# Moving SBUF tiles so that streamed weights start 64 bytes (mod 256) past the moving operand, in a two-layer hybrid decoder trunk

## The chip, the cores and the metric

The kernel runs on one core of one Trainium2 chip. The metric is device time in microseconds (us), the median of several executions. A profile of one further execution stands beside it.

## The reference

Two layers act on a sequence of 256 tokens of width 1024, in float32. Each layer is a half-step SwiGLU feed-forward, three parallel token mixers (differential attention, RWKV-7, HGRN2), and a second half-step SwiGLU, each on a normalized and modulated input:

```
for l in range(DEPTH):                                   # 2 layers
    mod = (silu(c) @ mod_w[l] + mod_b[l]).reshape(9, D)
    u = rms_norm(h, norm_w[l, 0]) * (1 + m[1]) + m[0]
    h = h + 0.5 * m[2] * (silu(u @ w_gate) * (u @ w_up)) @ w_down     # 1024 -> 2816 -> 1024
    u = rms_norm(h, norm_w[l, 1]) * (1 + m[4]) + m[3]
    p = u @ w_in[l]                                                    # 1024 -> 8480
    y = g_a * attention(p) @ w_out_a + g_b * rwkv7(p) @ w_out_b + g_c * hgrn2(p) @ w_out_c
    h = h + m[5] * (y @ w_out[l])
    u = rms_norm(h, norm_w[l, 2]) * (1 + m[7]) + m[6]
    h = h + 0.5 * m[8] * (second SwiGLU of u)
```

## The kernel before

Activations lie transposed, 128 features on the partitions and the 256 tokens along the row, so a matrix product is a chain of TensorE matmuls with a 128x128 block of weights as the stationary operand and a 128x256 block of activations as the moving operand. For precision each weight and each activation is split into a high and a low part (`split`, L364 to L366), and three of the four products are summed: helper `mm3` (L356 to L362) issues, for eight blocks k, high weights times high activations, high weights times low activations, and low weights times high activations, 24 matmuls in one accumulation. Nearly every matmul is followed by one with another block of weights, so a weight load (PEld in the profile) stands between any two; the load for the next matmul runs while the present one streams its moving operand.

Weights are never reused: `load` (L1323) brings 512 KB by the SP queue into one of four buffers `raw`, ScalarE makes `wh` (L365), VectorE makes `wl` (L366), three buffers each. The items are worked off in one fixed list: per layer the feed-forward (22 gate and 22 up blocks, then 8 down blocks in three pieces), the mixer's projections in the order of a string, its output projections and `w_out`, then the second feed-forward. Mixer work of other kinds is interleaved by a budget per item.

The moving operands of `mm3`, by their names in the profile:

- `zh`, `zl`: the activations before their normalization is known, 258 columns wide (two columns carry the shift), eight blocks in one tile, so a block starts 1,032 bytes after the one before. They serve the first items of each feed-forward and of each mixer.
- `uh`, `ul`: the normalized input, 256 columns (1,024 bytes) a tile, 3,072 of these passes' matmuls in the four feed-forwards and 1,920 in the two mixers.
- `hh`, `hl`: the hidden activations of a feed-forward, 528 matmuls in each.
- `oa`, `ob`, `oc`, then `yh`, `yl`: outputs of the three mixers and their gated sum; 192 matmuls each for the three, 384 for the sum.

In five projections (L945 to L947, `tm_proj`) the roles are exchanged: the activations are stationary and 512 columns of weights move.

SBUF tiles come from pools, stacked in the order in which they are opened: constants, residual and `zh`/`zl`, `stream` (`raw`, `wh`, `wl`), `tmp` (pool `tp`), and above it either pool `ff` of a feed-forward or pool `mx` of a mixer. In a pool, tiles lie in the order of their first use, each rounded up to 32 bytes. What a tile's address is mod 256 therefore follows from all that was placed ahead of it. In the built program every block of `wh` and `wl` starts at 224 mod 256.

Of the kernel before, what the change touches and what calls it, by code (L numbers as in the profile page):

```python
# [10 lines left out]
F32 = mybir.dt.float32  # L11
# [11 lines left out]
S = 256  # L23
KT = D // 128
# [6 lines left out]
NC = S // C  # L31
# [32 lines left out]
def trunk(ctx: ExitStack, tc: tile.TileContext, A, out):  # L64
# [6 lines left out]
    tp = ctx.enter_context(tc.tile_pool(name="tmp", bufs=2))  # L71
# [4 lines left out]
    def psd(w=S):  # L76
        return pd.tile([128, w], F32, name="psd", tag="psd")
# [27 lines left out]
    cos = cp.tile([128, 2, 32], F32, name="cos")  # L105
    sin = cp.tile([128, 2, 32], F32, name="sin")
    lam_init = [0.8 - 0.6 * math.exp(-0.3 * l) for l in range(L)]

    def col(l, n, i=0, w=1):
        o, _ = COLS[n]  # L110
        return cols[:, l, o + i:o + i + w]
# [138 lines left out]
    NOW = {}  # L250
# [92 lines left out]
    def mods_due(r, t=None):  # L343
        if t and mod_todo.index(t) < mod_pos[0]:
            return
        NOW["mods"] = NOW.get("mods", 0.0) + r
        while NOW["mods"] >= 1:
            NOW["mods"] -= 1
            mod_step()
# [65 lines left out]
    def z_close():  # L415
        with ahead(PRIO["z"]):
            z_sums()
# [14 lines left out]
    def z_rstd():  # L432
        pr = psm([128, S])
        PE.matmul(pr, ones, NOW["dg"].rearrange("p b t -> p (b t)"), start=True, stop=True)
        SC.copy(rstd, pr)
# [7 lines left out]
    def ffn_open():  # L443
        es = NOW["es"] = ExitStack()
        fp = NOW["ff"] = es.enter_context(tc.tile_pool(name="ff", bufs=1))
        cbc = NOW["cbc"] = fp.tile([128, D], F32, name="cbc")
        load_c(cbc)
# [15 lines left out]
    def ffn(l, i, nxt, per):  # L463
        s = 2 * i
        hid = [None] * FT
        pp = {}
        def gate_up(f, j, wh, wl):
            if f == 0 and j == 0 and (l or i):
                ffn_open()
            fp = NOW["ff"]  # L470
            if f >= (MODF if l + i else MODF0):
                mods_due(per[0])
            nz = NZ0 if l + i == 0 else NZ
            zt = f < nz
            if f == 0 and j == 0:
                NOW["z"] = [(NOW["zh"][:, k], NOW["zl"][:, k]) for k in range(KT)]
            n = 2 * f + j
            if n == 0:
                NOW["u"] = []
            if wh is None:  # L480
                p = NOW["pre"][n]
            else:
                p = psd(S + 2 if zt else S)
                mm3(p, wh, wl, NOW["z"] if zt else NOW["u"], late=n == 0)
                if n == 0:
                    z_close()
                elif n == 1:
                    z_rstd()
            if zt:
                make_u(l, s, fp, [k for k in range(KT) if (k * (2 * nz - 1)) // KT + 1 == n])  # L490
            pp[j] = p
            if j == 0:
                return
            pg, pu = pp[0], pp[1]
            t1 = fp.tile([128, S], F32, name="t1", tag="t1", bufs=2)
            t2 = fp.tile([128, S], F32, name="t2", tag="t2", bufs=2)
            if zt:
                bt = fp.tile([128, 1], F32, name="bt", tag="bt", bufs=2)
                V.tensor_copy(bt, pg[:, S:S + 1])
                V.tensor_mul(t1, pg[:, 0:S], rstd)  # L500
                SC.activation(t1, t1, AF.Silu, bias=bt)
                V.tensor_mul(t2, pu[:, 0:S], rstd)
                V.scalar_tensor_tensor(t2, t2, pu[:, S:S + 1], t1, ALU.add, ALU.mult)
            else:
                SC.activation(t1, pg, AF.Silu)
                V.tensor_mul(t2, t1, pu)  # L506
            a1 = fp.tile([128, S], F32R, name=f"hh{f}")
            a2 = fp.tile([128, S], F32R, name=f"hl{f}")
            split(a1, a2, t2)
            hid[f] = (a1, a2)  # L510

        def down(f, k0, kn, wh, wl):
            if f == 0 and k0 == 0:
                mod_until(l, 3 * s + 2)
                if nxt:
                    z_open(*nxt)
            if f < MODD:
                mods_due(per[1])
            if k0 == 0:
                pp[0] = psd()  # L520
            p = pp[0]
            mm3(p, wh, wl, hid[k0:k0 + kn], first=k0 == 0, last=k0 == 16)
            if k0 == 16:
                V.scalar_tensor_tensor(h[f], p, modd[:, l, 3 * s + 2, f:f + 1], h[f], ALU.mult, ALU.add)
                if nxt:
                    z_tile(*nxt, f)
                else:
                    nc.sync.dma_start(out[f], h[f])
                if f == KT - 1:
                    if i == 0:  # L530
                        mod_until(l, MODM[l])
                        NOW["ff"] = NOW["cbc"] = None
                    NOW["es"].close()

        for f in range(FT):
            for j in range(2):
                add(A["gu"][l, i, f, j], D, partial(gate_up, f, j))
        for f in range(KT):
            for k0, kn in ((0, 8), (8, 8), (16, 6)):
                add(A["dn"][l, i, f][:, k0 * 128:(k0 + kn) * 128], kn * 128, partial(down, f, k0, kn))  # L540
# [7 lines left out]
    def mixer(l):  # L548
        M = {}

        def tile_(shape, name, tag=None, dt=F32, bufs=None):
            kw = {} if bufs is None else {"bufs": bufs}
            return M["mx"].tile(shape, dt, name=name, tag=tag or name, **kw)


        def r_open():
            es = M["es"] = ExitStack()
            M["mx"] = es.enter_context(tc.tile_pool(name="mx", bufs=1))
            M["lw2"] = tile_([128, 512], "lw2", "Xa")
            GP.dma_start(M["lw2"], A["wa2"][l])  # L560
            GP.dma_start(rows, A["rows"][:, l * NROW:(l + 1) * NROW].to_broadcast([128, NROW]))
            M["u"] = None
            for n, t in (("rr", "r"), ("kk", "k"), ("aa", "a")):
                M[n] = tile_([128, 4, S], n, t)
            M["vv"] = tile_([128, 4, C + S], "vv", "v")
            M["Za"] = tile_([128, 2, NC, 2, 128], "Za")
            M["Zb"] = tile_([128, 2, NC, 2, 128], "Zb")
            M["H"] = tile_([128, 4, NC, 128], "H")
            M["EC"] = tile_([128, 4, NC], "EC")


        def shift_out(o, p, mi, b=None):
            ts = tile_([128, S + 1], "ts", bufs=2)
            if b is None:
                GP.memset(ts[:, 0:1], 0.0)
                SC.activation(ts[:, 1:S + 1], p, AF.Copy, scale=col(l, "mu", mi))
            else:
                SC.mul(ts[:, 0:1], b, omu[:, l, mi:mi + 1])
                SC.activation(ts[:, 1:S + 1], p, AF.Identity, scale=col(l, "mu", mi), bias=b)
            V.scalar_tensor_tensor(o, p, omu[:, l, mi:mi + 1], ts[:, 0:S], ALU.mult, ALU.add)  # L580
            return ts
# [6 lines left out]
        def proj(evac, wh, wl):  # L588
            n = M.setdefault("n", 0)
            M["n"] += 1  # L590
            zt = n < NZM
            if n == 0:
                r_open()
                drain("C")
                M["z"] = [(NOW["zh"][:, k], NOW["zl"][:, k]) for k in range(KT)]
                NOW["u"] = M["u"] = []
                M["wait"] = []
            mix_mods()
            p = psd(S + 2 if zt else S)
            mm3(p, wh, wl, M["z"] if zt else M["u"], late=n == 0)  # L600
            if n == 0:
                z_close()
            elif n == 1:
                z_rstd()
            if zt:
                make_u(l, 1, M["mx"], [k for k in range(KT) if (k * (NZM - 1)) // KT + 1 == n])
            M["wait"].append((evac, p))
            while n and M["wait"]:
                f, p = M["wait"].pop(0)
                bt = None  # L610
                if zt:
                    bt = tile_([128, 1], "bt", bufs=2)
                    SC.copy(bt, p[:, S:S + 1])
                    pn = tp.tile([128, S], F32, name="pn", tag="sq")
                    V.tensor_mul(pn, p[:, 0:S], rstd)
                    p = pn
                f(p, bt)
# [722 lines left out]
    z_open(0, 0)  # L1340
    step("C")
    pre = NOW["pre"] = [psd(S + 2) if i < 4 else psm([128, S + 2]) for i in range(NI)]
    zf = NOW["ff"].tile([128, KT, S + 2], F32, name="zf")
    zh, zl = NOW["zh"], NOW["zl"]
    raws = []
    for t in range(KT):
# [108 lines left out]
```

## Time and profile before

| | us |
|---|---|
| median of 3 timed executions | 1498.49 (1496.09 to 1505.21) |
| profiled execution, whole | 1506.07 |
| its span, first to last instruction | 1504.4 |
| TensorE matmul busy in it | 1449.7 (96%) |
| TensorE weight load busy | 1379.7 (92%) |
| VectorE busy | 1202.0 (80%) |
| ScalarE busy | 800.7 (53%) |
| GpSimd busy | 140.8 (9%) |

Busy time on PE is the union of modelled durations, and a matmul's modelled duration reaches over the start of the next. The time from one matmul's start to the next (its pace, below) is what a stream of matmuls costs; it comes from the length of a stretch in which PE is never idle, divided by the matmuls that start in it. A count in a stretch includes about two that began earlier and reach into it.

### The profile page before, as it was taken

How to read it: one execution, taken by the hardware profiler on the slowest of the kernel's cores; microseconds unless marked ns; L12 is line 12 of the kernel's file. 1: busy time of each engine (PE TensorE's matmuls, PEld its weight loads, DVE VectorE, ACT ScalarE, POOL GpSimd, SP SyncE). 2: the span in 40 equal slices, each digit the busy share in tenths (PEclk: the TensorE clock that was granted, in tenths of full speed). 3: DMA queues.
4: the chain of work that ended last, by engine and by line, in shares of the span. 5: the costliest groups of instructions: out<-in, count | busy, mean ns of one | idle time of the engine just before them, and what ended most of it. 6: DMA issues, size and time to landing. Idle time of an engine off the chain costs nothing. (4 is left out here: it accounts for less than half of the span.)

```text
span 1504.4 us, 30080 instructions
## 1 busy us (share of the span) xinstructions
PE 1449.7 (96%) x11848; PEld 1379.7 (92%) x11848; DVE 1202.0 (80%) x2228; ACT 800.7 (53%) x1367; POOL 140.8 (9%) x230
## 2 busy tenths in 40 slices
PE   4999999998999999999999999999979999999998
PEld 2999999997878999999999999999867789999998
DVE  5998988869779998888888888787778788886543
ACT  3564447863355656444455444688423664564432
POOL 6000010021300020000100000001222001100000
PEclk9999999999999999999999999999978999999999
DMA  9789975453326667899878997544541235665563
GB/s 329 260 271 344 319 272 176 129 173 118 116 84 197 204 205 269 287 308 308 260 267 297 327 329 256 186 141 141 164 144 46 85 127 181 200 210 184 181 189 118
DMA packets 90208, 315.92 MB, mean 210 GB/s; under 512 B 10577, under 2 KB 13009, under 8 KB 90066
## 3 DMA queue, kind: packets, MB, share of 16 engines
q1 hardware_dynamic: 86690, 308.32, 61.7%
q0 software_dynamic: 1600, 4.20, 1.1%
q8 instruction: 93, 1.52, 0.4%
q10 hardware_dynamic: 1776, 1.48, 0.3%
q14 instruction: 49, 0.40, 0.1%
HBM read 311.86 MB, written 2.10 MB: 209 GB/s over the span
## 5 line engine op out<-in xcount | busy, mean ns | idle before, releaser
L365 ACT CAST wh<-raw 128x1024 fp32r<-128x1024 f32 (+1 forms) x440 | 454.8, 1034 | 457.4 <-PE psd L362 258.0
L366 DVE TENSOR_TENSOR wl<-raw,wh 128x1024 fp32r<-128x1024 f32 (+1 forms) x440 | 533.7, 1214 | 124.8 <-ACT wh L365 119.4
L362 PE MATMUL psd<-uh,wl 128*128 128x256 f32 x1664 | 236.7, 284 | 16.6 <-DVE wl L366 16.6
L362 PE MATMUL psd<-uh,wh 128*128 128x256 f32 x1664 | 239.8, 285 | 0.0
L362 PE MATMUL psd<-ul,wh 128*128 128x256 f32 x1664 | 236.3, 284 | 0.0
L362 PEld LDWEIGHTS psd<-uh,wl 128*128 128x128 f32 x1664 | 215.0, 190 | 18.2 <-DVE wl L366 17.2
L362 PEld LDWEIGHTS psd<-uh,wh 128*128 128x128 f32 x1664 | 215.1, 189 | 4.3 <-issue 2.0
L362 PEld LDWEIGHTS psd<-ul,wh 128*128 128x128 f32 x1664 | 214.9, 190 | 0.5 <-issue 0.3
L314 DVE SCALAR_TENSOR_TENSOR mw<-mw,cbc 128x1024 f32<-128x1024 f32 x134 | 167.7, 1254 | 0.0
L362 PE MATMUL psd<-hl,wh 128*128 128x256 f32 x704 | 100.3, 282 | 0.0
L362 PE MATMUL psd<-hh,wl 128*128 128x256 f32 x704 | 100.0, 282 | 0.0
L362 PE MATMUL psd<-hh,wh 128*128 128x256 f32 x704 | 99.8, 282 | 0.0
L362 PEld LDWEIGHTS psd<-hl,wh 128*128 128x128 f32 x704 | 91.1, 188 | 0.0
L362 PEld LDWEIGHTS psd<-hh,wh 128*128 128x128 f32 x704 | 90.9, 188 | 0.0
L362 PEld LDWEIGHTS psd<-hh,wl 128*128 128x128 f32 x704 | 90.9, 188 | 0.0
L412 POOL TENSOR_TENSOR acc<-acc,sq 128x256 f32<-128x256 f32 x36 | 30.1, 835 | 605.3 <-ACT sq L410 605.0
L362 PE MATMUL psd<-zh,wh 128*128 128x258 f32 x448 | 66.0, 289 | 0.0
L946 PE MATMUL psd<-wl,uh 128*128 128x512 f32 x160 | 65.3, 408 | 0.6 <-DVE wl L366 0.6
L362 PE MATMUL psd<-zh,wl 128*128 128x258 f32 x448 | 64.9, 283 | 0.0
L506 DVE TENSOR_TENSOR t<-t,psd 128x256 f32<-128x256 f32 x64 | 26.9, 421 | 47.4 <-PE psd L362 46.5
L945 PE MATMUL psd<-wh,uh 128*128 128x512 f32 x160 | 64.7, 405 | 0.0
L947 PE MATMUL psd<-wh,ul 128*128 128x512 f32 x160 | 64.7, 404 | 0.0
(427 smaller groups left out, 2107.2 us busy)
## 6 DMA issues: line engine op xcount, KB each, us to landing
raw<-in_gu SPq DMA_DIRECT2D x176, 512.0 KB, 4.5
mw<-in_modw SPq DMA_DIRECT2D x134, 512.0 KB, 5.3
raw<-in_wfm SPq DMA_DIRECT2D x94, 512.0 KB, 3.6
raw<-in_dn SPq DMA_DIRECT2D x64, 512.0 KB, 4.7
raw<-in_wtm SPq DMA_DIRECT2D x40, 512.0 KB, 4.0
raw<-in_dn SPq DMA_DIRECT2D x32, 384.0 KB, 3.8
raw<-in_wo SPq DMA_DIRECT2D x24, 512.0 KB, 3.8
raw<-in_wout SPq DMA_DIRECT2D x16, 512.0 KB, 3.5
```

Of the source, the lines that this page charges most:

```text
L314: ins = V.scalar_tensor_tensor(w, w, 1.0, NOW["cbc"], ALU.mult, ALU.mult, accum_out=modd[:, l, j, f:f + 1])
L362: PE.matmul(p, w[:, sl[k]], xs[k][x], start=first and i == 0, stop=last and i == 3 * n - 1)
L365: SC.copy(dst_h, src)
L366: V.tensor_sub(dst_l, src, dst_h.bitcast(F32))
L412: GP.tensor_add(NOW["acc"], NOW["acc"], sq)
L506: V.tensor_mul(t2, t1, pu)
L945: PE.matmul(ps[b], u[k][0][:, ts_], w1, start=k == 0, stop=False)
L946: PE.matmul(ps[b], u[k][0][:, ts_], w2, start=False, stop=False)
L947: PE.matmul(ps[b], u[k][1][:, ts_], w1, start=False, stop=k == KT - 1)
```

## The change

The instructions and their order on every engine are the same before and after, row by row; only addresses change, and with them a few dependences that hang on what lay at an address earlier: the wait for a handful of long finished GpSimd-queue DMAs moves from the copy of `bt` to the neighbouring instruction on VectorE (twice) and from that copy to an activation on ScalarE (once).

Five edits shift tiles. An unused tile of 224 bytes, `gap`, opens pool `tmp`, so that everything behind it moves up by 224. The tiles `bt`, `ts` and `EC`, whose sizes are no multiples of 256 bytes, go from `ff` and `mx` into `tmp`. The tile `zf`, 8,256 bytes, is allocated with 8,448 bytes (33 times 256). And the name `PX` gets its 8,192 bytes when `mx` is opened instead of later.

```diff
+    tp.tile([128, 56], F32, name="gap", bufs=1)
...
-                bt = fp.tile([128, 1], F32, name="bt", tag="bt", bufs=2)
+                bt = tp.tile([128, 1], F32, name="bt", tag="bt")
...
-            M["EC"] = tile_([128, 4, NC], "EC")
+            M["EC"] = tp.tile([128, 4, NC], F32, name="EC", tag="EC", bufs=1)
+            tile_([128, 2, 4, S], "PX")
...
         def shift_out(o, p, mi, b=None):
-            ts = tile_([128, S + 1], "ts", bufs=2)
+            ts = tp.tile([128, S + 1], F32, name="ts", tag="ts")
...
-                    bt = tile_([128, 1], "bt", bufs=2)
+                    bt = tp.tile([128, 1], F32, name="bt", tag="bt")
...
-    zf = NOW["ff"].tile([128, KT, S + 2], F32, name="zf")
+    zf = NOW["ff"].tile([128, 33 * 64], F32, name="zf")[:, 0:KT * (S + 2)].rearrange("p (k s) -> p k s", k=KT)
```

The following table is counted from the addresses in the two built programs. For two consecutive matmuls of `mm3` it takes the distance, mod 256 bytes, from the moving block of the first to the weight block of the second, which is loaded while the first runs.

| moving operand | matmuls | distance before | distance after |
|---|---|---|---|
| `uh`, `ul` in the first feed-forward | 624 | 96 (seven blocks of eight), 160 (one) | 64 |
| `hh`, `hl` in the first feed-forward | 528 | 96 | 64 |
| `uh`, `ul` in the other three | 2,448 | 160 (seven blocks of eight), 224 (one) | 64 |
| `hh`, `hl` in the other three | 1,584 | 160 | 64 |
| `uh`, `ul` in the mixers | 1,920 | 32 (six of eight), 160 (two) | 64 |
| `yh`, `yl` | 384 | 32 (six of eight), 160 (two) | 64 |
| `ob` | 192 | 32 | 64 |
| `oc` | 192 | 64 | 64 |
| `oa` | 192 | 224 | 64 |
| `zh`, `zl` | 1,344 | 8 to 128 in steps of 8 | the same |
| weights, 512 wide (`tm_proj`) | 480 | 96 or 224 | 192 |

## The prediction

> **What bounds the kernel now.** The page comes first: which engine is busy, and whether at full clock.
>
> ```profile
> span 1504.4 us, 30080 instructions
> PE 1449.7 (96%) x11848; PEld 1379.7 (92%) x11848; DVE 1202.0 (80%) x2228; ACT 800.7 (53%) x1367; POOL 140.8 (9%) x230
> PE   4999999998999999999999999999979999999998
> DVE  5998988869779998888888888787778788886543
> PEclk9999999999999999999999999999978999999999
> DMA  9789975453326667899878997544541235665563
> ```
>
> PE is full in nearly every slice, at full clock except around slice 31. So the pace of its matmuls sets the time, and a change of addresses can act only there, as no instruction is added, removed or moved. The next view is the busy time in stretches with one kind of moving operand each: `zh` of the first feed-forward, its `uh`, its `hh`, then `uh` and `hh` of the second, `uh` of the third, `uh` and `hh` of the last, one `zh` stretch more.
>
> ```profile
> core 0: us, PE busy (x), PEclk, DMA share, GB/s
> 60.00:80.00 20.00, 20.00 (x169) 1.00 0.90 325
> 88.10:161.60 73.50, 73.50 (x625) 1.00 0.91 319
> 161.90:218.40 56.50, 56.50 (x478) 1.00 0.89 306
> 603.00:700.00 97.00, 97.00 (x814) 1.00 0.90 304
> 700.50:757.50 57.00, 57.00 (x478) 1.00 0.81 264
> 795.30:892.50 97.20, 97.20 (x816) 1.00 0.92 323
> 1339.50:1436.80 97.30, 97.30 (x817) 1.00 0.58 183
> 1437.00:1500.00 63.00, 63.00 (x527) 1.00 0.54 159
> ...
> 776.00:794.00 18.00, 18.00 (x151) 1.00 0.87 302
> ```
>
> PE never idles in any of them. Two of each count began earlier and are taken off; the length by the rest is the pace: 118.0 ns and 118.7 ns in the first feed-forward (`uh`, `hh`), 119.5, 119.7, 119.4, 119.4 and 120.0 in the later ones, 119.8 and 120.8 for `zh`. All are the same instruction at the same clock; what differs is where the operands lie, and the DMA share doesn't go with it (0.92 and 0.58 give the same 119.4). The same shape in the mixer's output projections stands in time order:
>
> ```profile
> 523.12 0.64 PE L362 MATMUL psd<-oc,wh 128*128 128x256 f32 x4
> ...
> 534.43 0.63 PE L362 MATMUL psd<-oa,wh 128*128 128x256 f32 x4
> ...
> 545.63 0.63 PE L362 MATMUL psd<-yh,wh 128*128 128x256 f32 x4
> ```
>
> From the first `oc` to the first `oa` are 11.31 us, from there to the first `yh` 11.20 us, each 96 matmuls (four items with two chains of 12): **117.8 ns** with `oc`, **116.7 ns** with `oa`. `oc` is the one operand that has the distance 64 already, with the same residues of moving tile (160) and weights (224) that the change gives to all. The 512-wide projection shows a floor:
>
> ```profile
> 326.65 0.40 PE L945 MATMUL psd<-wh,uh 128*128 128x512 f32 x1
> ...
> 349.05 0.41 PE L362 MATMUL psd<-uh,wh 128*128 128x256 f32 x2
> ```
>
> Between these starts lie 96 matmuls (eight items of twelve), 22.40 us, 233.3 ns each, twice the 116.7 of `oa`. There the weight load has twice the time to finish, and its distances (96 and 224) make no difference: 0.456 ns a column is what the moving operand itself takes. Whatever stands above 116.7 in a 256-wide stream comes with the distance: nothing at 224, 1.1 ns at 64, some 1.5 to 2 at 96, 2.7 to 3.3 at 160.
>
> A rule of the Trainium skill speaks against the change. "TensorE: Matmul & The Clock Gate", Part 2, says that TensorE reads the moving operand and the weights through two independent ports, so that loading the next weights takes no bandwidth from the running matmul. By it no distance would matter, and the sum below would be zero. The trace disagrees in part: 116.7 against 120.0 ns, with only tiles and addresses different.
>
> **The change part by part.** *The 256-wide streams.* I take 117.8 ns for all of them. Counts are from the page:
>
> ```profile
> L362 PE MATMUL psd<-uh,wl 128*128 128x256 f32 x1664 | 236.7, 284 | 16.6 <-DVE wl L366 16.6
> L362 PE MATMUL psd<-hl,wh 128*128 128x256 f32 x704 | 100.3, 282 | 0.0
> L362 PE MATMUL psd<-oa,wh 128*128 128x256 f32 x128 | 17.5, 279 | 0.0
> L362 PE MATMUL psd<-oc,wh 128*128 128x256 f32 x128 | 17.7, 281 | 0.0
> ```
>
> Three passes of 1,664 make 4,992 `uh`/`ul`: 624 in the first feed-forward, 3 x 816 in the others, 1,920 in the mixers. Three of 704 make 2,112 `hh`/`hl`, 528 a feed-forward. The mean of one in these rows points the same way, 279 for `oa`, 281 for `oc`, 282 and 284 for the rest. A stretch of `uh` in the mixer, from the same view as above:
>
> ```profile
> 1042.00:1049.00 7.00, 7.00 (x61) 1.00 0.58 182
> ```
>
> 7.00 us by 59 is 118.6 ns, and I use 118.5, since the stretch is short. The sum:
>
> - first feed-forward: 624 x 0.3 + 528 x 0.9 ns = 0.7 us;
> - `uh`, `ul` in the others: 2,448 x 1.65 = 4.0 us;
> - `hh`, `hl` in the others: 1,584 x 2.1 (119.9, the mean of their two stretches) = 3.3 us;
> - mixers: 1,920 x 0.7 = 1.3 us, `yh`, `yl` at the same 0.6: 0.2 us, `ob` 0.1 us;
> - `oa` loses 192 x 1.1 = 0.2 us.
>
> That is **9.4 us gained**. The bounds of the pace at 64 come from the nearest rows: 116.7 at best (the floor), which makes it 18 us, and 119.0 at worst (the mean of what runs now: 9.4 us over 7,872 matmuls above 117.8), which makes it 0. Two uneven spots are left in the value: `oc` blocks lie 1,024 bytes apart, `uh` and `hh` blocks 2,048 or 4,096, with the low tile and others between. The distance 96 shows a spread of 0.7 ns between two such layouts (118.0 and 118.7), so I allow 117.4 to 118.2 for the likeliest case: 6 to 13 us.
>
> *512-wide.* Their distance becomes 192, unseen here. They stand at the floor with 96 and 224 alike, so 0; a nanosecond each way would be 480 x 1 ns = 0.5 us.
>
> *`zh`.* Distances and addresses stay: 0.
>
> *Does the rest keep up?* An item in a feed-forward takes 24 x 119.4 ns = 2.87 us of PE now and 2.83 after. Beside it VectorE has, in the stretch from 603 to 700 us:
>
> ```profile
> L366 DVE TENSOR_TENSOR wl<-raw,wh 128x1024 fp32r<-128x1024 f32 x34 | 41.5, 1222 | 6.5 <-ACT wh L365 6.5
> L314 DVE SCALAR_TENSOR_TENSOR mw<-mw,cbc 128x1024 f32<-128x1024 f32 x24 | 29.2, 1217 | 0.0
> ...
> 603.00:700.00 97.00, 97.00 (x814) 97.00 (x813) 80.28 (x120) 46.82 (x69) 0.00 (x0) 1.00 0.90 304
> ...
> 795.30:892.50 97.20, 97.20 (x816) 97.20 (x815) 84.84 (x131) 47.25 (x70) 0.00 (x0) 1.00 0.92 323
> ```
>
> 80.3 of 97.0 us, and 84.8 of 97.2 in the third: 87%, which becomes 88.5% of 95.9 us. The DMA share of 0.92 becomes 0.93, at 327 GB/s; the stretch from 60 us moved 325. Both fit, narrowly for the DMA. If it can't give more than 323 GB/s, only the first and third feed-forward's `uh` stretches lose their gain, 1.5 us.
>
> *Small tiles.* `ts`, `bt` and `EC` have the same instructions on the same engines and keep their buffer counts:
>
> ```profile
> L575 POOL MEMSET ts<- x18: 98/98/103, 251.3 to 1012.6; 128x1 f32 x18
> ...
> L499 DVE COPY bt<-psd x23: 140/153/159, 51.4 to 1336.8; 128x1 f32<-128x1 f32 x23
> ...
> PE psd L362 <- DVE wl L366: 16.6, 3, 7.7
> ```
>
> The waits that pass from the copy of `bt` to its neighbour are for transfers of the mixer that ended long before a feed-forward begins: 0. Behind such a copy stand only VectorE's own next steps, and PE waits for VectorE in `mm3` three times in the whole program. `gap`, `zf` and `PX` cost no instruction.
>
> **The rivals.**
>
> 1. *No effect.* The distance mod 256 isn't what sets the pace, or the time comes back as PE's wait for DMA. For it: stretches with one distance still differ by 0.7 ns. Against: `oa` and `oc`, back to back on the same weights' buffers, differ by 1.1 ns. It gives 1498.5. The Trainium skill's rule of the two ports, quoted above from "TensorE: Matmul & The Clock Gate", Part 2, would end here too.
> 2. *The floor.* At 64 the streams run at 116.7, since the 1.1 ns of `oc` come from something of its own and not from the distance. For it: `oa`, with the same spacing of blocks, runs at 116.7. Against: `oa` has another distance, and both run beside the same weight casts. 18 us less: 1480.
> 3. *Slower.* At a block spacing of 2,048 or 4,096 bytes the distance 64 collides where `oc`'s 1,024 didn't. For it: `zh`, whose blocks are spaced differently again, has distances of 8 to 128, 64 among them, and the highest pace of all, 120.8. It decides from a pace of 119.0 on; at 120.8 it costs 7,872 x 1.8 = 14.2 us: 1513. Against: `uh` and `hh` at 96 with such spacings stay at 118.0 to 118.7.
>
> **How the numbers follow.** The profiled execution took 1506.07 us, 1.7 more than its span, and lies 7.6 above the median of the three timed ones, 1498.49; a gain in pace is the same in both, so the median falls to 1498.5 - 9.4 = **1489**. Chances: 0.66 for this, 0.13 for no effect, 0.13 for the floor, 0.08 for slower. The likeliest case spans 1485.5 to 1492.5, and some 4 us more each way, as the three executions spread by 9 us. Taking in no effect with its spread leaves out the floor and the slower case: **1481 to 1500**. A measurement of this kernel can hardly tell less than 1% (15 us) from no change. By over 1% faster is below 1483.5: the floor, and the upper edge of the likeliest case with luck in the spread, 0.19. Over 1% slower is most of the last rival, 0.05. The rest, 0.76, is within 1%.
>
> **What would show it.** In the profile after, `uh` stretches of 816 matmuls should last 96.1 us instead of 97.4, and `hh` of 528 62.2 instead of 63.4; `oc` stays at 11.31 us for 96, `oa` rises from 11.20 to the same 11.31; the 512-wide run stays at 22.4 us for 96, and `zh` stays. The prediction is wrong if `uh` and `hh` part from each other or from `oc` by over half a nanosecond, if they fall to 116.7, or if PE begins to wait for `wl` in the feed-forwards.

## The result, and the profile after

The changed kernel takes 1463.5 us (median of 4, 1463.3 to 1467.2) against 1498.0 us before (median of 4): a ratio of 0.976, interval 0.973 to 0.980. It is 34.5 us faster, far more than the 9.4 us of the forecast and outside the range of 1481 to 1500.

The page after, sections 1 and 2 (line numbers have moved: L364 is `mm3`, L948 to L950 are `tm_proj`):

```profile
span 1461.9 us, 30078 instructions
PE 1402.4 (96%) x11848; PEld 1334.1 (91%) x11848; DVE 1200.1 (82%) x2228; ACT 800.8 (55%) x1367; POOL 143.1 (10%) x230
...
PEclk9999999999899999999999999999989999999999
```

PE's busy time fell by 47 us with the same count of instructions, and VectorE's stayed. The stretches of one moving operand each (in the order of the rows: `uh`, `hh` of the first feed-forward; `uh`, `hh` of the second; `uh` of the third; `uh`, `hh` of the last; a `zh` stretch) in the view of busy time by window:

```profile
core 0: us, PE busy (x) PEld busy (x) DVE busy (x) ACT busy (x) POOL busy (x), PEclk, DMA share, GB/s
88.95:159.50 70.55, 70.55 (x625) 70.55 (x624) 67.08 (x127) 39.80 (x59) 0.00 (x0) 1.00 0.92 335
159.70:213.80 54.10, 54.10 (x480) 54.10 (x479) 52.46 (x77) 26.35 (x38) 4.41 (x5) 1.00 0.90 318
596.80:689.10 92.30, 92.30 (x817) 92.30 (x816) 80.03 (x120) 47.14 (x69) 0.00 (x0) 1.00 0.92 318
689.30:743.20 53.90, 53.90 (x478) 53.90 (x477) 46.01 (x70) 27.15 (x38) 4.47 (x5) 1.00 0.84 279
780.95:873.20 92.25, 92.25 (x817) 92.25 (x816) 84.05 (x131) 47.31 (x70) 0.00 (x0) 1.00 0.95 337
1305.55:1397.80 92.25, 92.25 (x816) 92.25 (x816) 56.99 (x77) 47.04 (x69) 0.00 (x0) 1.00 0.61 193
1398.00:1457.70 59.70, 59.70 (x529) 59.70 (x528) 28.23 (x31) 21.21 (x23) 0.00 (x0) 1.00 0.58 168
760.00:780.00 20.00, 20.00 (x168) 20.00 (x168) 19.50 (x41) 13.24 (x23) 0.00 (x0) 1.00 0.86 309
```

With two taken off each count as before (counting an edge more or less shifts the quotient by 0.2 ns), every `uh` and `hh` stretch runs at **113.3 ns**, where it was 118.0 to 120.0; `zh`, whose addresses keep their distance, runs at 120.5. `oc` and `oa`, by their starts in time order:

```profile
517.98 0.62 PE L364 MATMUL psd<-oc,wh 128*128 128x256 f32 x4
...
528.86 0.62 PE L364 MATMUL psd<-oa,wh 128*128 128x256 f32 x4
...
539.74 0.50 PE L364 MATMUL psd<-yh,wh 128*128 128x256 f32 x3
```

10.88 us for 96 matmuls in both: 113.3 ns. `oc` had the distance 64 before too, and ran at 117.8.

Where the time went: the four feed-forwards' `uh` and `hh` streams are 3.0 + 2.8 + 3 x (5.0 + 3.5) = 31.3 us shorter (624, 528, 816 and 528 steps at the old pace less 113.3; the last 48 `hh` steps of each of the first three, behind a short break, stay near 118, which takes 0.6 us off). The first layer's mixer, from its `zh` streams to the next feed-forward's first `uh`, gives 1.7 us (stretch, its length, PE busy with its count, clock, DMA share, GB/s):

```profile
232.70:602.80 370.10, 356.40 (x2951) 0.98 0.52 166
```

before, and after

```profile
228.20:596.60 368.40, 352.09 (x2951) 0.98 0.52 167
```

PE needs 4.3 us less there, but idles 16.3 us instead of 13.7: the mixer's chains through other engines set part of its time. The second mixer is 11.5 us shorter (375.3 us before, 363.8 after), but most of that isn't the change's: the two profiled spans differ by 42.5 us, 8 more than the medians, and that is the clock in the profiled execution of before, between 1120 and 1160 us of its second mixer:

```profile
1120.00:1160.00 40.00, 39.03 (x440) 0.79 0.15 50
```

against 1.00 at that place after. A fifth of 40 us is 8 us.

### The profile page after: what moved, and what is told of

Its sections match the earlier page's. It is cut to its first block, busy times and chain, and to the rows that moved or that the text cites. A ratio compares the mean times of both kernels' runs of the same rounds, so it can differ in the third digit from the quotient of the medians.

```text
span 1461.9 us, 30078 instructions
## 1 busy us (share of the span) xinstructions
PE 1402.4 (96%) x11848; PEld 1334.1 (91%) x11848; DVE 1200.1 (82%) x2228; ACT 800.8 (55%) x1367; POOL 143.1 (10%) x230
## 5 line engine op out<-in xcount | busy, mean ns | idle before, releaser
L367 ACT CAST wh<-raw 128x1024 fp32r<-128x1024 f32 (+1 forms) x440 | 455.7, 1036 | 414.0 <-PE psd L364 241.2
L364 PE MATMUL psd<-uh,wl 128*128 128x256 f32 x1664 | 229.8, 280 | 18.5 <-DVE wl L368 18.5
L364 PE MATMUL psd<-uh,wh 128*128 128x256 f32 x1664 | 232.2, 280 | 0.0
L364 PE MATMUL psd<-ul,wh 128*128 128x256 f32 x1664 | 227.8, 279 | 0.0
L364 PEld LDWEIGHTS psd<-uh,wl 128*128 128x128 f32 x1664 | 209.1, 191 | 20.0 <-DVE wl L368 19.1
L364 PEld LDWEIGHTS psd<-uh,wh 128*128 128x128 f32 x1664 | 208.4, 189 | 4.3 <-issue 2.0
L364 PEld LDWEIGHTS psd<-ul,wh 128*128 128x128 f32 x1664 | 207.4, 189 | 0.5 <-issue 0.3
L364 PE MATMUL psd<-hl,wh 128*128 128x256 f32 x704 | 96.1, 277 | 0.0
L364 PE MATMUL psd<-hh,wl 128*128 128x256 f32 x704 | 95.9, 277 | 0.0
L364 PE MATMUL psd<-hh,wh 128*128 128x256 f32 x704 | 95.6, 276 | 0.0
L364 PEld LDWEIGHTS psd<-hh,wl 128*128 128x128 f32 x704 | 87.3, 188 | 0.0
L364 PEld LDWEIGHTS psd<-hl,wh 128*128 128x128 f32 x704 | 87.2, 188 | 0.0
L364 PEld LDWEIGHTS psd<-hh,wh 128*128 128x128 f32 x704 | 87.1, 188 | 0.0
L364 PE MATMUL psd<-zh,wh 128*128 128x258 f32 x448 | 65.8, 288 | 0.0
L364 PE MATMUL psd<-zh,wl 128*128 128x258 f32 x448 | 65.6, 286 | 0.0
L948 PE MATMUL psd<-wh,uh 128*128 128x512 f32 x160 | 64.2, 401 | 0.0
L950 PE MATMUL psd<-wh,ul 128*128 128x512 f32 x160 | 64.0, 400 | 0.0
L364 PE MATMUL psd<-zl,wh 128*128 128x258 f32 x448 | 63.9, 283 | 0.0
```

The lines of the kernel that those rows point to most:

```text
L364: PE.matmul(p, w[:, sl[k]], xs[k][x], start=first and i == 0, stop=last and i == 3 * n - 1)
L367: SC.copy(dst_h, src)
L948: PE.matmul(ps[b], u[k][0][:, ts_], w1, start=k == 0, stop=False)
L950: PE.matmul(ps[b], u[k][1][:, ts_], w1, start=False, stop=k == KT - 1)
```

## The experiments

After the result stood the question why 64 gives 113.3 in all streams when `oc` at 64 had shown 117.8. Theory A: at one distance the chain of loads and matmuls can repeat in more than one pattern, each with its own pace, and what starts the stream decides which. Theory B: any distance does, as long as all are equal, or each pair pays its own price. Theory C: 113.3 belongs to where the tiles of the changed kernel lie.

**One distance for all, its value varied.** The size of `gap` moves all moving blocks together:

```diff
-    tp.tile([128, 56], F32, name="gap", bufs=1)      # 224 bytes: distance 64
+    tp.tile([128, 16], F32, name="gap", bufs=1)      # 64 bytes: 224; likewise 8: 0; 40: 128; 24: 192; none: 32
```

> The unused tile `gap` has 64 bytes instead of 224, so every 256-wide pair stands at distance 224 instead of 64, all else as after. Theory A (each distance has its own repeating patterns, and the fast one of 113.3 ns belongs to 64): the `uh` and `hh` stretches run at the 116.7 ns that `oa` showed before, 816 `uh` last 95.2 us, the span is about 1462 + 8,000 x 3.4 ns = 1489 us. Theory B (what counts is that all distances are equal, whichever): 113.3 ns and a span of 1462 us.

> `gap` of 32 bytes: distance 0 for every 256-wide pair. Theory A: no row of before shows it; weights and moving block start on the same residue, so the worst or near it, 118 to 125 ns, span 1500 to 1555 us. Theory B: 113.3 ns, 1462 us.

> `gap` of 160 bytes: distance 128 for every 256-wide pair. Theory A: between the neighbours of before, 118.2 (96) and 119.9 (160), so about 119 ns and a span of about 1462 + 8,000 x 5.7 ns = 1508 us. Theory B: 113.3 ns, 1462 us.

> `gap` of 96 bytes: distance 192 for every 256-wide pair. Theory A: between 119.9 (160) and 116.7 (224), about 118 ns, span about 1500 us. Theory B: 113.3 ns, 1462 us.

> No `gap` tile: distance 32 for every 256-wide pair, the one left out of the series beside 96 and 160, which before had in `hh` streams (118.7 and 120.0). `ob` had it before and ran at 118.2. Theory A: a repeating pattern at about 118.2, or a slower one up to 120, span 1495 to 1510 us. Rival: 113.3 as next to 64.

Measured: 1481.9 us at 224, 1504.7 at 0, 1504.1 at 128, 1479.1 at 192, 1499.2 at 32, one execution each. The paces are what is compared. Stretches of `uh` at 224, in the second and the last feed-forward:

```profile
597.20:693.10 95.90, 95.90 (x817) 1.00 0.89 307
...
1319.40:1414.40 95.00, 95.00 (x816) 1.00 0.59 188
```

117.7 and 116.7 ns, the same instructions at the same addresses in two feed-forwards. At 0 and at 128 (`uh` of the first and of the second feed-forward):

```profile
608.90:706.50 97.60, 97.60 (x816) 1.00 0.89 301
```

```profile
88.40:162.20 73.80, 73.80 (x625) 1.00 0.90 319
603.10:700.80 97.70, 97.70 (x816) 1.00 0.89 301
```

119.9 at 0; 118.5 and 120.0 at 128. At 192, `uh` of all four feed-forwards in order:

```profile
88.50:159.00 70.50, 70.50 (x624) 1.00 0.92 333
597.40:693.30 95.90, 95.90 (x817) 1.00 0.91 307
787.20:879.50 92.30, 92.30 (x817) 1.00 0.95 340
1315.10:1411.00 95.90, 95.90 (x816) 1.00 0.59 186
```

113.3, 117.7, 113.3, 117.7 ns. At 32:

```profile
602.30:698.60 96.30, 96.30 (x817) 1.00 0.89 306
```

118.2 ns. Even distances alone don't give 113.3, so Theory B's first form falls. The levels are few and exact, and one distance can have two of them, in one execution. Theory A's order was right at 224 (the 116.7 of `oa`, in half of the long streams), at 0, at 32 and at 128; 192 was expected at 118 and has the fast level as well.

**The gap alone.**

```diff
 # the kernel before
+    tp.tile([128, 56], F32, name="gap", bufs=1)
```

> The kernel before with the tile `gap` of 224 bytes alone; the small tiles stay in their pools and `zf` keeps its size. Distances become 192 for `uh` (seven of eight) and `hh` of the three later feed-forwards, 128 for those of the first, 64 (six of eight) for the mixers' `uh`. Theory A (repeating patterns by distance, kept as long as the distance is the same from pair to pair): `hh` of the later feed-forwards runs at 113.3 or 117.8 ns as in the run at 192, but `uh`, with one block of eight elsewhere, at no such pattern, 117 to 120; `hh` of the first at 118.7 or 120.0. Span 1480 to 1500 us. Theory B (each pair pays by its own distance alone, averaged): `uh` within 0.5 ns of `hh`.

Measured: 1490.0 us. `uh` and `hh` of the second feed-forward:

```profile
603.70:699.30 95.60, 95.60 (x816) 1.00 0.90 307
699.60:755.50 55.90, 55.90 (x477) 1.00 0.82 269
```

117.4 ns with one block of eight at another distance, 117.7 without. Both theories allowed this: it doesn't tell them apart. In this one execution the shift by itself brought some 7 of the 34 us. Its `hh` streams, at 192, sat in the slower level of that distance, so how the gain divides between the shift and the edits that make the distances alike is not settled.

**One block of eight moved off.**

```diff
-            uh = pool.tile([128, S], F32R, name=f"uh{k}")
-            ul = pool.tile([128, S], F32R, name=f"ul{k}")
+            odd = k == 0 and pool is NOW["ff"]
+            uh, ul = (pool.tile([128, S + 64 * odd], F32R, name=f"{n}{k}")[:, 16 * odd:S + 16 * odd] for n in ("uh", "ul"))
```

> The kernel after, with block 0 of `uh` and `ul` in the feed-forwards starting 64 bytes later, so that three pairs of 24 stand at distance 0; `hh` and the mixers keep 64 throughout. Theory A: the odd block breaks the pattern in each pass, and `uh` runs well above the mean of its pairs, 116 to 119 ns, while `hh` stays at 113.3 or 117.8. Theory B (each pair pays its own): `uh` at (21 x 113.3 + 3 x 120.0)/24 = 114.2 ns, `hh` at 113.3.

Measured: 1480.9 us. `uh` and `hh` of the second feed-forward:

```profile
598.30:693.30 95.00, 95.00 (x816) 1.00 0.89 309
693.50:747.30 53.80, 53.80 (x477) 1.00 0.84 279
```

`uh` at 116.7, `hh` right behind at 113.3. Three odd pairs of 24 cost 24 x 3.3 = 80 ns a pass of 24, four times what they would cost by their own price (3 x 6.7 = 20 ns). By the starts in the trace, of each eight matmuls the first four follow one another at 118 to 124 ns and the other four at 113 to 114. Theory B's second form falls: the odd block slows its neighbours.

**A disturbance behind each item.** A tiny fp32 matmul of one column, its result unused, in the last feed-forward:

```diff
+    def jolt():
+        PE.matmul(psm([128, 2])[:, 0:1], ident, ones[:, 0:1], start=True, stop=True)
...
+            if l and i and n >= 2 * NZ:
+                jolt()
...
             mm3(p, wh, wl, hid[k0:k0 + kn], first=k0 == 0, last=k0 == 16)
+            if l and i:
+                jolt()
```

> The kernel after, with one tiny fp32 matmul, its result unused, behind each item of the last feed-forward from its `uh` stretch on. Theory A (at distance 64 a stream can repeat in a pattern of 113.3 or in one of 117.8 ns, and what starts it decides): behind the tiny matmuls some items run at 113.3 and some at 117.8, with hardly anything between; the stretch lasts longer by the tiny matmuls (about 0.5 us each, 58 of them) and by up to 4.4 ns x 1,340. Theory C (113.3 belongs to the addresses of `after`, and what `oc` showed before came from where it lay then): every item returns to 113.3.

Measured: 1485.5 us. L367 is the tiny matmul; two passes of eight ahead of one, in the last feed-forward:

```profile
1382.86 1.07 PE L364 MATMUL psd<-ul,wh 128*128 128x256 f32 x8
...
1384.67 0.28 PE L367 MATMUL psm<-ones,ident 128*128 128x1 f32 x2
```

1.81 us for 16 matmuls: 113.1 ns. After some slower first steps every full item of 24 came back to 113.3, not some: this one kind of start led to the one pattern, and the mix that Theory A expected didn't come. But Theory C falls on the same trace, whose first and second mixer run `oc` at the same addresses:

```profile
517.09 0.39 PE L364 MATMUL psd<-oc,wh 128*128 128x256 f32 x2
...
527.97 0.50 PE L364 MATMUL psd<-oa,wh 128*128 128x256 f32 x3
...
1237.18 0.40 PE L364 MATMUL psd<-oc,wh 128*128 128x256 f32 x2
...
1248.49 0.40 PE L364 MATMUL psd<-oa,wh 128*128 128x256 f32 x2
```

10.88 us and 11.31 us for the 96: 113.3 and 117.8 ns. The latter is what `oc` showed before the change. And up to the last feed-forward this kernel has the instructions and the addresses of the changed kernel, where the second mixer's `oc` ran otherwise:

```profile
1229.78 0.50 PE L364 MATMUL psd<-oc,wh 128*128 128x256 f32 x3
...
1240.66 0.50 PE L364 MATMUL psd<-oa,wh 128*128 128x256 f32 x3
```

10.88 us, 113.3 ns. So the level isn't fixed by the program: in a mixer at least, the same stream can have either in different executions.

**One disturbance ahead of a long stream.** At distance 192, where both levels occurred:

```diff
+            if n == 2 * nz - 1:
+                jolt()
```

> The run at distance 192 with a single tiny fp32 matmul, its result unused, at the end of each feed-forward's `zh` items. At 192 two feed-forwards (first, third) ran at 113.3 ns and two (second, last) at 117.8. Theory A (two patterns at one distance, and the first steps of a stream decide which it keeps): the start is now the same in all four, so all four run at one level; behind the same matmul at distance 64 that was the fast one, so `uh` and `hh` of the second and last come down to 113.3, 2 x 1,344 x 4.4 ns = 12 us less for 1 us of tiny matmuls, span about 1466 us. Theory C (the level belongs to the place in the program or the addresses): second and last stay at 117.8, span 1478 us.

Measured: 1486.4 us. `uh` of the third and last feed-forward:

```profile
788.20:884.10 95.90, 95.90 (x816) 1.00 0.92 327
1322.30:1418.30 96.00, 96.00 (x816) 1.00 0.58 186
```

117.7 ns in both, and in the second too. In the first, PE had done the tiny matmul long before its stream began at 90 us (first of the eight, counting two for each, in the answer by line), and it stayed at 113.3:

```profile
L367 PE MATMUL psm<-ones,ident x8: 166/208/250, 52.1 to 1322.1; 128*128 128x1 f32 x8
```

So the direction was missed: with the tiny matmul directly ahead, all three streams ran in the slow pattern. In the third feed-forward the next 1,344 matmuls stood at 117.7 where they had 113.3 without it, 6 us. That the tiny matmul did this fits Theory A, but it isn't shown: each kernel was profiled in one execution, and a level can change between executions of the same instructions, as `oc` did above.

**All addresses moved, distances kept.**

```diff
+    hp.tile([128, 8], F32, name="lead")
     hall = hp.tile([128, KT, S], F32, name="h")
```

> The kernel after with an unused tile of 32 bytes ahead of all activations and weights, so that weights and moving blocks both start 32 bytes later (0 and 192 mod 256 instead of 224 and 160) and every distance is kept, that of `zh` too. If only the distance counts: `uh` and `hh` at 113.3 (or at 117.8 where a stream starts otherwise), span 1462 us. If the residue itself counts (a start on a multiple of 64 against one 32 past it): another level, somewhere from 113 to 120 ns.

Measured: 1464.4 us, as after. `uh` and `hh` of the second feed-forward:

```profile
597.30:689.60 92.30, 92.30 (x817) 1.00 0.91 318
689.80:743.70 53.90, 53.90 (x478) 1.00 0.83 278
```

113.3 ns. A shift of weights and activations by the same 32 bytes changes nothing. The moving blocks start at 192 mod 256 here, as in the run at 32, which ran at 118.2 with weights at 224: it is the distance that counts, not where the moving block starts.

**Extending the change to `zh`.** 

```diff
-        NOW["zh"] = hp.tile([128, KT, S + 2], F32R, name="zh", tag="ZH")
-        NOW["zl"] = hp.tile([128, KT, S + 2], F32R, name="zl", tag="ZL")
+        NOW["zh"] = hp.tile([128, KT * 320], F32R, name="zh", tag="ZH").rearrange("p (k s) -> p k s", k=KT)[:, :, 0:S + 2]
+        NOW["zl"] = hp.tile([128, KT * 320 + 16], F32R, name="zl", tag="ZL")[:, 0:KT * 320].rearrange("p (k s) -> p k s", k=KT)[:, :, 0:S + 2]
...
-MWB = 6
+MWB = 5
...
-                t = tile_([128, S], f"gt{i}")
+                t = tile_([128, S], f"gt{i}", {8: "lw", 9: "cs", 10: "xx", 11: "Ep"}.get(i))
```

> The kernel after, with the blocks of `zh` and `zl` 1,280 bytes apart instead of 1,032, and both tiles placed so that their pairs stand at 64 too. Paid for with one buffer of `mw` less (five) and four gate tiles sharing places with tiles that are dead by then. Theory A: `zh` streams of 258 columns run at 258/256 x 113.3 = 114.2 ns instead of 120.5 (or at 118.7 in the slow pattern), 1,344 of them: 8.5 us less than after, about 1455 us, if five buffers of `mw` are enough. Theory B expects the same here. Theory C (113.3 belongs to the addresses of `after`): `zh` and, as all tiles lie elsewhere, the others too may come out anywhere between 113 and 120 ns.

Measured: 1478.0 us (median of 4, 1462.0 to 1487.0), ratio to before 0.984, interval 0.976 to 0.991. It doesn't beat the change. Two `zh` items in time order, then `uh` of the second and the last feed-forward:

```profile
584.34 0.40 PE L364 MATMUL psd<-zh,wh 128*128 128x258 f32 x2
...
587.22 0.40 PE L364 MATMUL psd<-zh,wh 128*128 128x258 f32 x2
```

```profile
598.80:691.10 92.30, 92.30 (x816) 1.00 0.91 319
1310.40:1406.30 95.90, 95.90 (x817) 1.00 0.60 186
```

`zh` runs at 120.0 ns here even at distance 64 (2.88 us for 24), and at 120.8 in the first and the last feed-forward by the same trace, so Theories A and B missed it; and the last feed-forward falls into 117.7, at distance 64. Three of its four executions took 1462.0, 1474.5 and 1481.4 us; levels that differ from one to the next would fit that, but only one was profiled.

**`zh` without its two extra columns.**

```diff
-                NOW["z"] = [(NOW["zh"][:, k], NOW["zl"][:, k]) for k in range(KT)]
+                NOW["z"] = [(NOW["zh"][:, k, 0:S], NOW["zl"][:, k, 0:S]) for k in range(KT)]
...
-                mm3(p, wh, wl, NOW["z"] if zt else NOW["u"], late=n == 0)
+                V.memset(p[:, S:S + 2], 0.0) if zt else None
+                mm3(p[:, 0:S], wh, wl, NOW["z"] if zt else NOW["u"], late=n == 0)
```

(on top of the edit before, and likewise in the mixer's `proj`; it leaves out the shift that the two columns carry)

> The kernel with padded `zh` and `zl` (all pairs at distance 64), but `zh` streams are 256 columns wide instead of 258: the two columns that carry the shift are left out, and VectorE writes zeros in their place, so this part of the result is missing. Theory A: the width of 258 is what keeps `zh` from a repeating pattern, so at 256 `zh` runs at 113.3 or 117.8 ns instead of 121. Rival: something else about `zh` (float32r written by ScalarE just before, its early place) makes it slow, and it stays at 119 to 121 ns.

Measured: 1493.2 us, with VectorE's extra writes and the stalls that they cause. Items of `zh` in the first feed-forward (three between these rows) and in the second (two):

```profile
71.57 0.50 PE L364 MATMUL psd<-zh,wh 128*128 128x256 f32 x3
...
79.73 0.39 PE L364 MATMUL psd<-zh,wh 128*128 128x256 f32 x2
...
583.05 0.40 PE L364 MATMUL psd<-zh,wh 128*128 128x256 f32 x2
...
588.70 0.28 PE L364 MATMUL psd<-zh,wh 128*128 128x256 f32 x1
```

8.16 us for 72 is 113.3 ns, 5.65 us for 48 is 117.7: the two levels of distance 64. So the width of 258 kept `zh` from them; the one other difference from the run before is VectorE's writes.

## Why the prediction was wrong

The step that failed is the value taken for the pace at distance 64, "I take 117.8 ns for all of them", and the bound below it, "116.7 at best (the floor)". In their place the runs showed two levels at that distance, 113.3 and 117.8 ns, and in the long streams of the changed kernel the faster.

- *117.8 from `oc`.* The reading of the row was right, the step from one stream to the distance was not. 117.8 is one of two levels at 64, and `oc`, started behind `ob` streams at another distance, happened to sit in the slower; that both of its streams before did was bad luck for the forecast. The same `oc` ran at 113.3 and at 117.8 in one execution of the run with the disturbances. The stretches at 113.3 make the feed-forwards' term 31.3 us instead of 8.0.
- *The floor.* I took it from the 512-wide run, 233.3 ns, twice 116.7. The 512-wide streams too have several levels. After the change (distance 192) 16 of them lie between these starts:

```profile
443.56 0.39 PE L950 MATMUL psd<-wh,ul 128*128 128x512 f32 x1
...
447.22 0.39 PE L948 MATMUL psd<-wh,uh 128*128 128x512 f32 x1
```

  3.66 us, 228.8 ns each, below the supposed floor. In the run at distance 0 the same kind of stream settles lower still: 18 of them from 477.55 to 481.63 us, 226.7 ns each, which is twice 113.3. What two streams have in common needn't be a limit.
- *The rivals.* "No effect" and "slower" didn't come. "The floor" was the right direction, bounded by the wrong number. Its reason, that the 1.1 ns of `oc` weren't the distance's own, was nearer to the truth than the forecast, and it got 0.13.
- *The spread between layouts* (118.0 against 118.7 at 96) was put down to block spacing and widened the pace by 0.4 ns. The 118.7 is one of the exact levels, and `uh` at 118.0 has a block of eight off it; a few exact values that return were the hint that I took for noise. (The 119.8 and 120.8 of `zh` are one level, 120.5, read from short stretches with an edge more or less.)
- *Right:* PE sets the time, and nothing else broke. VectorE kept up (84.05 of 92.25 us in the third `uh` stretch, 91%), and so did the DMA (0.95 at 337 GB/s, above the 323 that I had feared as a limit). `zh` stayed, and no wait of PE's for one of the small tiles appears. Of the 4.3 us that PE saved in the first mixer 2.6 went into waits.
- *The port rule* of the Trainium skill ("TensorE: Matmul & The Clock Gate", Part 2), by which loading the next weights takes no bandwidth from the running matmul, would have the distance make no difference. That isn't borne out here: from distance 0 to distance 64 the same streams go from 120.0 to 113.3 ns. What collides no run shows.

## What to carry to other kernels

Where PE streams one matmul per weight load, the distance between the moving operand and the next weights is worth a sweep: a single unused tile of varied size at a pool's start does it, once all moving tiles have the same residue. Read the pace from long stretches, and look for several exact levels at one setting, in more than one execution, before a level is used as the price of that setting. A forecast from one stream's level needs the other levels as its bounds.

## What the runs showed of the hardware

Paces of 256-wide fp32r matmuls, each with another weight block, full clock, by the distance of the next weights past the moving block (of the runs at 0, 32, 128 and 224 one execution was profiled, so a second level there may have gone unseen):

| distance mod 256 | ns a matmul | from |
|---|---|---|
| 0 | 120.0 | all streams of that run |
| 32 | 118.3 | all streams of that run |
| 64 | 113.3 or 117.8 | after; mixers |
| 96 | 118.7 | `hh` of the first feed-forward before |
| 128 | 118.7 or 120.0 | feed-forwards of that run |
| 160 | 120.0 | `hh` of the others before |
| 192 | 113.3 or 117.8 | feed-forwards of that run |
| 224 | 116.7 or 117.8 | feed-forwards of that run |

A stream keeps its level for over 1,300 matmuls until something interrupts it or the distances vary. In the changed kernel's mixers, where small matmuls cut in, both levels stand a few microseconds apart, 24 matmuls between each pair of starts:

```profile
258.66 0.40 PE L364 MATMUL psd<-uh,wh 128*128 128x256 f32 x2
...
261.49 0.40 PE L364 MATMUL psd<-uh,wh 128*128 128x256 f32 x2
...
271.44 0.39 PE L364 MATMUL psd<-uh,wh 128*128 128x256 f32 x2
...
274.16 0.50 PE L364 MATMUL psd<-uh,wh 128*128 128x256 f32 x3
```

2.83 us (117.9 ns) and 2.72 us (113.3 ns). Open are what in the two reads collides, why 64 and 192 have the fastest level, and what in a start selects the level: at 64 all eight long feed-forward streams of the changed kernel fell into the fast one, with `zh` padded only six of them, and at 192 half. The gain of the change therefore rests on the starts as well as on the distance.
